# A bias tile loaded as overlapping rows of a table and read backwards, in a one-layer hybrid decoder

## The chip, the core and the metric

The kernel runs on one core of one Trainium2 chip. The metric is the device time of one execution in microseconds, taken as the median over several runs. A core has five engines that run side by side and synchronise with semaphores: TensorE (PE in the profile, with PEld for its weight loads), VectorE (DVE), ScalarE (ACT), GpSimd (POOL) and SyncE (SP). SP and POOL issue the DMA transfers of this kernel; all transfers share 16 DMA engines.

## The reference

One layer of a decoder is computed for 256 tokens of width 1024, in float32. Cut to what matters here:

```python
def hybrid_mixer(x, w_in, b_in, conv_qk, mlstm_norm, rel_bias, w_branch_a, w_branch_b, w_out):
    proj = einsum("bsd,dn->bsn", x, w_in) + b_in
    q_m, k_m, v_m, o_m, i_m, f_m, q_b, k_b, v_b, g_a, g_b = split(proj)
    ...                                            # mLSTM branch (4 heads x 256) -> y_a
    h_b = moba_attention(q_b, k_b, v_b, rel_bias)  # 8 heads x 128 -> y_b
    merged = sigmoid(g_a) * (y_a @ w_branch_a) + sigmoid(g_b) * (y_b @ w_branch_b)
    return merged @ w_out

# with 256 tokens and a block of 256, each query attends its own block only:
rel_own   = q_pos[:, None] - k_pos[None, :]
bias_own  = moveaxis(rel_bias[t5_bucket(rel_own)], -1, 0)     # depends on q_pos - k_pos and the head
logit_own = einsum("bhqd,bhkd->bhqk", q, k) * 128 ** -0.5 + bias_own
logit_own = where(rel_own >= 0, logit_own, -inf)
h_b       = softmax(logit_own) @ v

x = layer_norm(ALPHA * x + mix, ln1_g, ln1_b)
x = layer_norm(ALPHA * x + conv_gated_mlp(x), ln2_g, ln2_b)
```

The bias of a pair of query and key depends on their distance alone, so for one head it is a row of 256 numbers, and a query further on sees that row shifted by one.

## The kernel before

**Weights.** All weights are streamed from DRAM in chunks of 128 x 2048 float32 (1 MB), in the order that `chunk_order` (L45) writes out. Each chunk is split by ACT and DVE (L93, L94) into a rounded part `wh` and a remainder `wl`, and PE makes every product as three matmuls (L147): high by high, low by high, high by low. The main loop (L342) takes one chunk a step: `elem_work(s)` puts the elementwise work of the step on ACT, DVE and POOL, with the split of chunk s + 2 among it; `load(s + 5)` issues a later chunk on SP; then `step_<kind>` issues the chunk's matmuls, and after them the small matmuls of `side_pe`. The order of instructions on each engine is the order in which the program writes them.

**Groups.** The mixer runs in four groups of one mLSTM head and two attention heads. A group has eight chunks (qm, qb, km, kb, vm, vb, ga, gb), and its small work is laid between them by `group_schedule` (L644). For a group that begins at chunk b, the steps that matter here are (groups 0 to 2):

- after the matmuls of chunk b + 5 (vb): the mLSTM scores `pss` (L653) and the logits `psl` of the first head (L755);
- with chunk b + 6 (ga), in this order: `el_w` (L665: ACT makes the decay weights `wt` from the row `nMb`, POOL masks them), `el_l(0)` (L770: DVE adds the bias to the logits and takes the row maximum, L779), the split of vb into `vbh` and `vbl` (L531), `el_e(0)` (ACT's exponentials, L788), `el_s` (L676: scores times weights, ACT's rounded part `sph`), `el_l2(0)` (L790: division by the row sum), `el_s2` (L687: the remainder `spl`);
- after the matmuls of chunk b + 6: the logits of the second head, and `psn` (L691), the mLSTM product, which needs `sph` and `spl`;
- with chunk b + 7 (gb): `el_l(1)` and its followers, and after its matmuls the transposes `pst` of both heads' probabilities (L796).

The last group has the same pieces one step earlier.

**The bias.** `rel_bias_expand` (L554) makes, once, a matmul of the bias table with a one-hot matrix. Its result `ps` (8 heads x 256) holds at column j the bias for distance 255 - j. `elem` copies it, divided by the logit scale, into `ev` (8 x 384), fills the last 128 columns with -1e30 (keys that lie ahead of the query), and stores `ev` as the DRAM tensor `table`.

Each group then needs a tile `toe` of 128 partitions x 2 heads x 256 keys, in which row p is the table's row shifted by p. `copy_band` (L401) writes 128 copies of a table row of 384 behind one another into a DRAM tensor `band`, and `load_band` (L406) reads that back with a row length of 383, so that each row begins one element earlier in its copy. Both are issued on POOL, and the load waits for the copy. Copy and load of group 0 stand right behind the store of `table`. The copy for group g + 1 stands behind the elementwise work of group g's chunk ga; the load for group g + 1, into the same tile `toe`, stands with the second chunk of group g + 1, behind the logits of group g.

**Names in the profile.** L566 is the store of `table`, L403 the copies, L408 the loads, L779 the logits' bias, L672 POOL's mask, L731 POOL's power for the mLSTM norm.

Of the kernel before, what the change touches and what calls it, by code (L numbers as in the profile page):

```python
# [10 lines left out]
F32 = mybir.dt.float32  # L11
# [3 lines left out]
ALU = mybir.AluOpType  # L15
# [3 lines left out]
P = 128  # L19
S = 256  # L20
D = 1024
KT = D // P
NG = 4
# [6 lines left out]
ATT_SCALE = 128.0 ** -0.5  # L30
NEG = -1.0e30
LTOE = 384
# [40 lines left out]
class Kernel:  # L73
# [105 lines left out]
    def run(self):  # L179
        tc, nc, ctx = self.tc, self.nc, self.ctx  # L180
# [3 lines left out]
        dram = ctx.enter_context(tc.tile_pool(name="dram", bufs=1, space=DRAM))  # L184
# [106 lines left out]
        g = nc.gpsimd  # L291
# [34 lines left out]
        for gi in range(NG):  # L326
            self.group_schedule(gi)

        self.bands = [dram.tile([2, P * LTOE], F32, name=f"band{i}") for i in range(NG)]
        self.table = dram.tile([8, LTOE], F32, name="table")  # L330
        self.mrows = dram.tile([4, S], F32, name="mrows")

# [65 lines left out]
        self.pt = [(ap.tile([P, 2, P], F32R, name=f"pth{i}"), ap.tile([P, 2, P], F32R, name=f"ptl{i}"),  # L398
                    ap.tile([P, P], F32, name=f"ptf{i}")) for i in range(2)]

    def copy_band(self, g):  # L401

        self.nc.gpsimd.dma_start(self.bands[g].rearrange("h (p c) -> h p c", p=P),  # L403
                                 self.table[2 * g:2 * g + 2, :].unsqueeze(1).to_broadcast([2, P, LTOE]))

    def load_band(self, g):  # L406
        src = self.bands[g][:, 127:127 + P * (LTOE - 1)].rearrange("h (p c) -> p h c", c=LTOE - 1)
        self.nc.gpsimd.dma_start(self.toe, src[:, :, 0:S])  # L408


    def step_o(self, whl, bo):
# [142 lines left out]
    def rel_bias_expand(self, rel, onehot):  # L554
        nc = self.nc
        st = {}

        def pe():
            st["ps"] = ps = self.ps_side([8, S], "ps_rel")
            nc.tensor.matmul(ps, rel, onehot, start=True, stop=True)  # L560

        def elem():
            ev = self.xp.tile([8, LTOE], F32, name="ev")
            nc.vector.tensor_scalar(ev[:, 0:S], st["ps"], 1.0 / ATT_SCALE, None, op0=ALU.mult)
            nc.vector.memset(ev[:, S:LTOE], NEG)
            nc.gpsimd.dma_start(self.table, ev)  # L566
            self.copy_band(0)
            self.load_band(0)
        self.side_pe.setdefault(4, []).append(pe)
        self.side_elem.setdefault(5, []).append(elem)  # L570
# [73 lines left out]
    def group_schedule(self, g):  # L644
        nc = self.nc
        v, a = nc.vector, nc.scalar
        st = {}
# [122 lines left out]
        def el_l(i):  # L770
            h = 2 * g + i
            ps = st["l", i]
            lg = self.ap.tile([P, 3, P], F32, tag="lg", name=f"lg{h}", bufs=2)
            mx = self.ap.tile([P, 2], F32, tag="mx", name=f"mx{h}", bufs=2)
            sm = self.ap.tile([P, 2], F32, tag="sm", name=f"sm{h}", bufs=2)
            seg = ((lg[:, 0, :], ps[:, 0, 0:P], self.toe[:, i, P:2 * P]),
                   (lg[:, 1:3, :].rearrange("p t c -> p (t c)"), ps[:, 1, :], self.toe[:, i, :]))
            for t, (o, p, tb) in enumerate(seg):
                v.tensor_tensor_reduce(out=o, in0=p, in1=tb, scale=ATT_SCALE, scalar=-3.0e38, op0=ALU.add, op1=ALU.max,  # L779
                                       accum_out=mx[:, t:t + 1])  # L780
            v.tensor_scalar(mx, mx, -1.0, None, op0=ALU.mult)
            st["p", i] = lg
            st["m", i] = seg, mx, sm
# [46 lines left out]
        def at(where, k, f):  # L830
            where.setdefault(b + k, []).append(f)

        if g:
            at(self.side_elem, 1, lambda: self.load_band(g))
        if g < NG - 1:
            at(self.side_elem, 6, lambda: self.copy_band(g + 1))

        o = int(g < NG - 1)
        at(self.side_elem, 3 + o, row_m)
# [4 lines left out]
        if o:  # L844
            self.mixed[b + 6] = lambda w: [el_w, lambda: el_l(0), w[0], lambda: el_e(0), el_s, lambda: el_l2(0),
                                           el_s2] + w[1:]
        else:
            self.mixed[b + 5] = lambda w: [w[0], el_w, lambda: el_l(0), w[1], lambda: el_e(0), el_s,
                                           lambda: el_l2(0), el_s2] + w[2:]
        if g == 0:  # L850
            at(self.side_elem, 6, lambda: self.floor_exp())
        at(self.side_pe, 6 + o, lambda: pe_t(0))
        at(self.side_pe, 6 + o, lambda: pe_t(1))
        self.mixed[b + 6 + o] = lambda w: [lambda: el_l(1), lambda: el_e(1), el_n1] + w + [lambda: el_l2(1), el_n1b]
        at(self.side_pe, 7 + o, pe_y)
        at(self.side_pe, 7 + o, pe_o)
# [445 lines left out]
```

## Time and profile before

| | us |
|---|---|
| median of 3 runs | 485.36 |
| the runs | 491.53, 485.36, 484.46 |
| the profiled execution, whole | 489.01 |
| its span | 487.3 |
| PE busy in the span | 475.9 |
| DVE busy | 371.1 |
| ACT busy | 298.1 |
| POOL busy | 28.8 |

The profile is of one execution. Its span runs from the first to the last instruction, and 1.71 us of that execution lie outside it. Rows of a timeline give the start in us, the length in us, engine, line, operation, output and inputs by the program's names with their shapes, the number of merged instructions, and in brackets the idle time of the engine before them with what ended it. Rows of the chain give start, length and what ran; "issue" is time in which the profile shows no wait that was ended by anything. Rows by stretches give the busy time of PE, PEld, DVE, ACT and POOL with the number of instructions, then the clock that TensorE was granted (1.00 is full), the mean busy share of the DMA engines and GB/s. Rows of DMA issues give the median time from issue to landing last. The starts of PE's matmuls are measured and their ends are modelled, so that one row can reach into the next.

The memory traffic of the bias is small beside the weights: 94.31 MB were moved in all, of which the four copies write 384.0 KB each and the four loads 256.0 KB each.

### The profile page before, as it was taken

Reading aid. Unit: us, or ns where it says so; the run is one execution under the profiler, and the core shown is the slowest. Engines: PE = TensorE matmul, PEld = TensorE weight load, DVE = VectorE, ACT = ScalarE, POOL = GpSimd, SP = SyncE. Lnnn points to the kernel's source line nnn. Section 1 sums busy time; section 2 is a strip of 40 time slices with the busy share of each in tenths; the row PEclk is TensorE's granted clock in tenths of the full one; section 3 lists DMA queues with packets and bytes.
Section 4 is the critical chain, followed back from the end, with each engine's and each line's share of the span. In section 5 each row is a group of like instructions: output and inputs, shape, how many; then the busy total and the mean of one; then the engine's idle time right before and its main releaser. Section 6 shows DMA issues by size and latency. Waiting matters only on the chain.

```text
span 487.3 us, 9421 instructions
## 1 busy us (share of the span) xinstructions
PE 475.9 (98%) x3831; PEld 460.2 (94%) x3831; DVE 371.1 (76%) x666; ACT 298.1 (61%) x509; POOL 28.8 (6%) x45
## 2 busy tenths in 40 slices
PE   7999989999999999999999999999999999999994
PEld 5999989999999999999999999999999999999984
DVE  5779948796779686986666799888677667767886
ACT  5579656686569656867655541776445554556871
POOL 0501012001100110001100002000000000000000
PEclk9999998999999999999999999999999999999998
DMA  7976664466435754544875480736554565555202
GB/s 226 290 303 239 199 235 134 168 231 217 166 145 210 239 157 153 202 169 162 319 284 174 174 310 38 297 136 225 208 178 174 204 223 173 174 196 230 93 1 87
DMA packets 21030, 94.31 MB, mean 194 GB/s; under 512 B 4947, under 2 KB 7905, under 8 KB 11129
## 3 DMA queue, kind: packets, MB, share of 16 engines
q1 hardware_dynamic: 16714, 87.61, 50.2%
q0 software_dynamic: 4272, 6.09, 4.0%
q8 instruction: 30, 0.49, 0.4%
q14 instruction: 14, 0.11, 0.1%
HBM read 92.59 MB, written 2.64 MB: 195 GB/s over the span
## 4 chain that ended last, share of the span: by engine, by line
PE 83%; DMA 6%; issue 4%; DVE 3%; ACT 1%; SPq 1%; POOL 0%; DVEq 0%; ACTq 0%; POOLq 0%
PE ps_up L147 25%; PE ffn L147 12%; PE ps_gb L147 5%; PE mix L147 4%; PE ps_wb L147 4%; PE ps_wa L147 4%; PE ps_ga L147 3%; PE ps_kb L147 3%; PE ps_qm L147 3%; PE ps_qb L147 3%; PE ps_vm L147 3%; PE ps_vb L147 3%; PE ps_km L147 3%; DMA raw<-in_wst_dram 3%; DMA xraw<-in_xt_dram 2%
## 5 line engine op out<-in xcount | busy, mean ns | idle before, releaser
L94 DVE TENSOR_TENSOR wl<-raw,wh 128x1024 fp32r<-128x1024 f32 (+4 forms) x147 | 179.3, 1257 | 26.9 <-ACT wh L93 24.2
L93 ACT CAST wh<-raw 128x1024 fp32r<-128x1024 f32 (+4 forms) x147 | 151.7, 1080 | 8.5 <-DMA raw<-in_wst_dram 6.1
L147 PE MATMUL ps_up<-x1h,wl 128*128 128x256 f32 x320 | 88.5, 276 | 0.0
L147 PE MATMUL ps_up<-x1h,wh 128*128 128x256 f32 x320 | 88.4, 276 | 0.0
L147 PE MATMUL ps_up<-x1l,wh 128*128 128x256 f32 x320 | 88.4, 276 | 0.0
L147 PEld LDWEIGHTS ps_up<-x1l,wh 128*128 128x128 f32 x320 | 60.1, 188 | 0.4
L147 PEld LDWEIGHTS ps_up<-x1h,wh 128*128 128x128 f32 x320 | 60.1, 188 | 0.3
L147 PEld LDWEIGHTS ps_up<-x1h,wl 128*128 128x128 f32 x320 | 60.1, 188 | 0.0
L1080 DVE SCALAR_TENSOR_TENSOR cu<-ps_up,vec,cu 128x255 f32<-128x255 f32 (+1 forms) x80 | 33.0, 475 | 20.4 <-ACT cu L1076 20.4
L147 PE MATMUL ffn<-wh,hl 128*128 128x512 f32 (+2 forms) x94 | 35.5, 378 | 0.0
L147 PE MATMUL ffn<-wl,hh 128*128 128x512 f32 (+2 forms) x94 | 35.5, 377 | 0.0
L147 PE MATMUL ffn<-wh,hh 128*128 128x512 f32 (+2 forms) x94 | 35.3, 375 | 0.0
L93 ACT CAST hh<-cu 128x256 fp32r<-128x256 f32 x22 | 8.9, 406 | 40.4 <-DVE cu L1091 40.4
L1076 ACT ACTIVATE cu<-ps_up,vec 128x256 f32<-128x256 f32 x40 | 16.7, 470 | 22.5 <-PE ps_up L147 22.5
L147 PEld LDWEIGHTS ffn<-wh,hl 128*128 128x128 f32 x94 | 17.7, 188 | 3.2
L147 PEld LDWEIGHTS ffn<-wh,hh 128*128 128x128 f32 x94 | 17.7, 188 | 3.1
L147 PEld LDWEIGHTS ffn<-wl,hh 128*128 128x128 f32 x94 | 17.7, 188 | 3.0
L147 PE MATMUL ps_gb<-xth,wh 128*128 128x256 f32 x64 | 18.0, 282 | 0.0
L147 PE MATMUL ps_qm<-xth,wh 128*128 128x256 f32 x64 | 18.0, 281 | 0.0
L147 PE MATMUL ps_ga<-xth,wh 128*128 128x256 f32 x64 | 18.0, 281 | 0.0
L147 PE MATMUL ps_gb<-xtl,wh 128*128 128x256 f32 x64 | 17.9, 280 | 0.0
L147 PE MATMUL mix<-wh,mgh 128*128 128x256 f32 x64 | 17.8, 279 | 0.0
(344 smaller groups left out, 1454.6 us busy)
## 6 DMA issues: line engine op xcount, KB each, us to landing
raw<-in_wst_dram SPq DMA_DIRECT2D x77, 1024.0 KB, 4.9
raw<-in_wst_dram SPq DMA_DIRECT2D x8, 256.0 KB, 4.3
lnrow<-in_rows_dram POOLq DMA_DIRECT2D x4, 512.0 KB, 6.5
band<-table POOLq DMA_DIRECT2D x4, 384.0 KB, 11.2
xraw<-in_xt_dram SPq DMA_DIRECT2D x8, 128.0 KB, 4.0
toe<-band POOLq DMA_DIRECT2D x4, 256.0 KB, 4.6
xtok<-in_x_dram POOLq DMA_DIRECT2D x1, 1024.0 KB, 7.8
sgb<-in_wst_dram SPq DMA_DIRECT2D x4, 128.0 KB, 4.1
```

The lines of the kernel that those rows point to most:

```text
L93: self.nc.scalar.copy(wh, raw)
L94: self.nc.vector.tensor_sub(wl, raw, wh.bitcast(F32))
L147: self.nc.tensor.matmul(ps, a[i], b[i], start=start and i == 0, stop=stop and i == 2)
L1076: act.activation(cu[:, j, :], ps[:, j, :], AF.Copy, scale=tap(2, j))
L1080: v.scalar_tensor_tensor(cu[:, j, o:], ps[:, j, :S - o], tap(t, j), cu[:, j, o:], op0=ALU.mult, op1=ALU.add)
```

## The change

The copies in DRAM are gone. `ev` is built the other way round: its first 128 columns are -1e30, and column 128 + m holds the bias for distance m, which DVE gets by reading the matmul's result backwards in PSUM. `load_band` reads `table` itself: partition p gets the 256 elements from column 1 + p on, for both heads, so that the 128 rows overlap in all but one element each. That tile has the keys in reversed order: element 255 - k of row p is the bias for distance 128 + p - k, which is query 128 + p and key k. The new helper `backward` makes a view with step -1 over 256 elements, and `el_l` gives this view of `toe` to the logits instruction; the first query block takes the last 128 elements of the view, as before.

The store of `table` on POOL is followed directly by the load of group 0. The loads of groups 1 to 3 stay where they were. Sizes, numbers and order of all other instructions are as before.

```diff
-        self.bands = [dram.tile([2, P * LTOE], F32, name=f"band{i}") for i in range(NG)]
         self.table = dram.tile([8, LTOE], F32, name="table")
...
-    def copy_band(self, g):
-
-        self.nc.gpsimd.dma_start(self.bands[g].rearrange("h (p c) -> h p c", p=P),
-                                 self.table[2 * g:2 * g + 2, :].unsqueeze(1).to_broadcast([2, P, LTOE]))
+    def backward(self, t):
+        return bass.AP(t.tensor, t.offset + S - 1, [list(t.ap[0]), [-1, S]])

     def load_band(self, g):
-        src = self.bands[g][:, 127:127 + P * (LTOE - 1)].rearrange("h (p c) -> p h c", c=LTOE - 1)
-        self.nc.gpsimd.dma_start(self.toe, src[:, :, 0:S])
+        t = self.table[2 * g:2 * g + 2, 1:S + 1].unsqueeze(0)
+        rows = bass.AP(t.tensor, t.offset, [[1, P], *t.ap[1:]])
+        self.nc.gpsimd.dma_start(self.toe, rows)
...
             ev = self.xp.tile([8, LTOE], F32, name="ev")
-            nc.vector.tensor_scalar(ev[:, 0:S], st["ps"], 1.0 / ATT_SCALE, None, op0=ALU.mult)
-            nc.vector.memset(ev[:, S:LTOE], NEG)
+            nc.vector.tensor_scalar(ev[:, P:LTOE], self.backward(st["ps"]), 1.0 / ATT_SCALE, None, op0=ALU.mult)
+            nc.vector.memset(ev[:, 0:P], NEG)
             nc.gpsimd.dma_start(self.table, ev)
-            self.copy_band(0)
             self.load_band(0)
...
-            seg = ((lg[:, 0, :], ps[:, 0, 0:P], self.toe[:, i, P:2 * P]),
-                   (lg[:, 1:3, :].rearrange("p t c -> p (t c)"), ps[:, 1, :], self.toe[:, i, :]))
+            toe = self.backward(self.toe[:, i, :])
+            seg = ((lg[:, 0, :], ps[:, 0, 0:P], toe[:, P:2 * P]),
+                   (lg[:, 1:3, :].rearrange("p t c -> p (t c)"), ps[:, 1, :], toe))
...
-        if g < NG - 1:
-            at(self.side_elem, 6, lambda: self.copy_band(g + 1))
```

## The prediction

> **What bounds the kernel now.** I read the page's head first, then busy time by stretches (span, then busy us of PE, PEld, DVE, ACT, POOL; PEclk; DMA share; GB/s), then the chain that ended last, then each engine's timeline around the one place where PE stops.
>
> ```profile
> span 487.3 us, 9421 instructions
> PE 475.9 (98%) x3831; PEld 460.2 (94%) x3831; DVE 371.1 (76%) x666; ACT 298.1 (61%) x509; POOL 28.8 (6%) x45
> ```
> ```profile
> 65.00:71.00 6.00, 6.00 (x54) 5.95 (x53) 1.01 (x7) 2.21 (x4) 2.15 (x3) 1.00 0.75 240
> 71.00:74.00 3.00, 0.85 (x4) 0.41 (x2) 2.06 (x7) 2.55 (x8) 0.00 (x0) 0.88 0.14 54
> 74.00:76.00 2.00, 2.00 (x9) 2.00 (x10) 1.86 (x2) 1.06 (x2) 0.00 (x0) 0.50 0.12 51
> ...
> 94.00:480.00 386.00, 386.00 (x3148) 375.96 (x3147) 298.29 (x515) 235.65 (x392) 15.23 (x20) 1.00 0.52 186
> ```
> From 94 to 480 us PE is busy for 386.00 of 386.00 us at full granted clock: nothing that shortens other engines there can shorten the kernel. The exception is 71 to 76: PE works 0.85 us of 3, and the next 2 us are granted a clock of 0.50. The chain (start, length) says whose fault it is:
>
> ```profile
> 47.77 1.12 POOL band L403
> 48.89 15.95 issue
> 64.86 5.21 DMA toe<-band
> ...
> 71.09 0.34 DVE vbl L94
> ...
> 73.40 0.56 DVE spl L689
> 73.96 0.04 issue
> 74.00 1.87 PE psn L147 x7
> 75.88 5.91 PE ps_gb L147 x48
> 81.79 0.65 PE pst L799 x6
> ```
> ```profile
> 124.34 0.22 PE psl L760 x2
> 124.56 1.07 PE psn L147 x9
> 125.63 5.46 PE ps_gb L147 x48
> 131.09 0.65 PE pst L799 x6
> ```
> The 15.95 us of "issue" are the flight of the first band copy. The copy and the load after it bring the first bias tile at 70.07 us; DVE's logits wait for it, the chain ends in psn, and PE stands. Group 1 (second fence) has the same PE work without that wait.
>
> ```profile
> 62.92 2.36 DVE L94 TENSOR_TENSOR wl<-raw,wh 128x1024 fp32r<-128x1024 f32 x2 [0.25 <-ACT wh L93]
> 70.24 0.29 DVE L779 CUSTOM_DVE_ANT_0 lg<-psl,toe 128x128 f32<-128x128 f32 x1 [4.96 <-DMA toe<-band]
> ```
> ```profile
> 64.72 0.38 PE L760 MATMUL psl<-kbf,qbf 128*128 128x128 f32 x2
> ```
> ```profile
> 70.76 0.38 PE L760 MATMUL psl<-kbf,qbf 128*128 128x128 f32 x2
> 73.16 0.49 PE L147 MATMUL psn<-vmh,sph 128*128 128x258 f32 x1 [2.01 <-ACT sph L683]
> ```
> DVE is idle for 4.96 us before the logits; its own work was done at 62.92 + 2.36 = 65.28, and PE's logits product at 64.72 + 0.38 = 65.10.
>
> **The change part by part.** *The first copy goes.* The load of the first tile takes the copy's place in POOL's queue, at 47.77, behind the same table store. What the load costs there, with overlapping rows as source, has no row. Its nearest rows (KB, us from issue to landing):
>
> ```profile
> lnrow<-in_rows_dram POOLq DMA_DIRECT2D x4, 512.0 KB, 6.5
> band<-table POOLq DMA_DIRECT2D x4, 384.0 KB, 11.2
> ```
> ```profile
> band<-table POOLq DMA_DIRECT2D x1, 384.0 KB, 16.8
> ```
> Lower bound: 5.2, the load of before (5.21 in the chain; the same destination, size and row length). Upper bound: 16.8, the slowest copy out of the same table in the very stretch where the load will now run. I take 5.2 to 6.5, since lnrow too has all partitions read the same few KB; landing is at 53.0 to 54.3. Even 16.8 gives 47.77 + 16.8 = 64.6, before 65.28. So the logits start at 65.28 at every price between the bounds; a slower reversed PSUM read into ev (or its memset, which only moves) has the same 11 us of cover.
>
> *What is late next.* DVE runs logits, vbl, scores, spl in that order.
>
> ```profile
> 66.87 0.35 ACT L93 CAST vbh<-ps_vb 128x256 fp32r<-128x256 f32 x1
> ```
> ```profile
> 67.09 0.42 POOL L672 TENSOR_SCALAR_AFFINE_SELECT wt<-wt 128x256 f32<-128x256 f32 x1 [1.48 <-ACT wt L671]
> ```
> The logits took 71.09 - 70.24 = 0.85, so they end at 66.13. vbl needs vbh, at 67.22; the scores need the mask, at 67.51. If vbl starts at 67.24, and vbl to the end of spl keeps its length of 73.96 - 71.09 = 2.87, spl is there at 70.1. PE finishes the second logits product at 70.76 + 0.22 = 70.98 (two issues took 0.22 in group 1). So psn's operands are 0.9 us early, and PE has no wait. That is the margin on which the forecast stands.
>
> *The sum.* psn starts at 70.98. In group 1 psn's start to pst's start takes 131.09 - 124.56 = 6.53. So pst starts at 77.51 instead of 81.79: **4.28 us** less, of which 2.18 is the gap (73.16 - 70.98) and 2.10 the wait inside psn and the matmuls at the lower clock. Behind it PE has no waits, so the whole tail moves with it. Weights don't object: the split that DVE does next is of the weights two chunks ahead, and it moves up with spl.
>
> ```profile
> 74.14 2.36 DVE L94 TENSOR_TENSOR wl<-raw,wh 128x1024 fp32r<-128x1024 f32 x2 [0.19 <-ACT wh L93]
> ```
>
> On that clock the Trainium skill, "TensorE: Matmul & The Clock Gate", Part 1, says the clock drops after an idle window of about 3.4 us. The trace disagrees: 0.50 was granted right behind a gap of 2.2 us. Were the rule right, the low clock would have another cause and could stay; that is the second rival below.
>
> *The other copies and loads.* Three later copies (L403) leave POOL and the DMA engines. Nothing waits for them: the next tile's load is
>
> ```profile
> 82.04 0.90 POOL L408 DMA_DIRECT2D toe<-band  x1
> ```
> and its reader comes a whole group later, past 118. Cover is over 30 us, so both the copies and the new loads count nothing, even at 16.8.
>
> *Reversed reads of the bias tile*, 16 instructions (min/median/max ns), no row of before reads backwards:
>
> ```profile
> L779 DVE CUSTOM_DVE_ANT_0 lg<-psl,toe x16: 282/356/422, 70.2 to 217.9; 128x128 f32<-128x128 f32 x8, 128x256 f32<-128x256 f32 x8
> ```
> ```profile
> 46.62 0.68 DVE L608 TENSOR_TENSOR_SCAN gates<-ones,gates 4x256 f32<-4x256 f32 x1
> ```
> Lower bound: unchanged, 0.28 and 0.42 us (0.14 us for 128 columns more, 1.1 ns a column; a gain has no room, as the PSUM operand is still read forwards at one column a step). Upper bound: the slowest DVE row over 256 columns, the scan, 0.68 against 0.42: about 1.6 times, +0.43 us for a pair. I take unchanged, since the pace is a column at a time already. At the upper bound it is hidden too: in group 0 the pair ends at 66.6, before vbh; in the others DVE normalises its logits well before PE transposes them (group 1: 126.92 + 0.55 = 127.47 against 131.09, 3.62 us):
>
> ```profile
> 126.92 0.55 DVE L794 TENSOR_SCALAR lg<-lg,sm 128x128 f32<-128x128 f32 x2
> ```
>
> Sum: span 487.3 - 4.28 = 483.0. The profiled execution took 489.01, 1.71 outside the span; 484.7 after. The median of the runs shown is 485.36 (484.46 to 491.53), so against it the forecast is **481.1 us**, 0.9% less.
>
> **Rivals.** *Late load.* POOL's load now starts while DVE is full, where the old load started with DVE idle:
>
> ```profile
> 47.80:61.30 13.50, 13.50 (x122) 13.50 (x120) 13.38 (x24) 9.05 (x16) 1.09 (x1) 1.00 0.65 218
> 65.30:70.10 4.80, 4.80 (x45) 4.80 (x44) 0.00 (x0) 1.91 (x4) 1.85 (x3) 1.00 0.79 265
> ```
> If POOL's load only gets on when DVE goes idle (65.28), it lands 5.2 us later, at 70.5, against 70.07: before's time, no gain, 485.4. For it: the copy in the busy stretch was the slowest, 16.8. Against it: the copy did land while DVE was busy. It decides from a landing later than 66.4 + 0.9 = 67.3 (vbl needs 67.24 and 0.85 of logits before it), 19.5 us after issue; no row is that long. The Trainium skill, "SBUF — State Buffer", Who interferes with whom, states such a block of POOL's descriptor writing, but only by DVE's two-port modes; no run here shows which. Chance 0.08.
>
> *Half the gain.* Either the low clock of 74 to 76 comes anyway, or another operand of psn (ACT's chain behind the nMb row, with 0.9 us to spare) is late: only about the gap's 2.18 is won, 483.2. Against: groups 1 to 3 run the same work at full clock without a wait. Chance 0.10.
>
> *Slower: reversed reads cost several times as much.* Each pair of reads (0.28 + 0.42) grows by x, and a group has two in line ahead of the transposes. A group then loses 2x less its cover: 3.62 in groups 1 to 3 (group 3 taken like 1), in group 0
>
> ```profile
> 78.66 0.55 DVE L794 TENSOR_SCALAR lg<-lg,sm 128x128 f32<-128x128 f32 x2
> ```
> 79.21, moved by the 3.86 that spl moves (73.96 to 70.1) to 75.35, against pst at 77.51: 2.16. Together 8x - 13.0. The gain of 4.28 is eaten at x = 2.16, a pair four times as long; over 2% slower needs x = 3.4. At six times, x = 3.5: 28.0 - 13.0 = 15.0 lost, 485.36 - 4.28 + 15.0 = 496.1. For it: no row reads backwards. Against: the slowest row is 1.6 times. Chance 0.04.
>
> *It doesn't do what it says*: the first load is held on POOL by a wait that the diff doesn't show, up to about 64.86, where the old load was issued: 485.4, chance 0.03. Against it: in the diff the load reads only the table, and DVE had not read that tile before.
>
> **How the numbers follow.** Forecast 0.75, rivals 0.08, 0.10, 0.04, 0.03. The forecast's own range is 479.7 to 482.5: 0.9 to each side, by which the two closest runs shown differ (485.36 - 484.46), and 0.1% (0.5) more, since three runs are few. The whole range reaches on through half a gain (483.2) to no gain with the same 0.5, 479.7 to 485.9, and leaves out the slow rival (0.04). About 2% (9.7 us) is what a measurement of this kernel can tell from no change: no case reaches -9.7, so faster 0.02; the slow rival, partly, gives slower 0.04; within 0.94.
>
> **What would show it.** Right: toe lands near 53; DVE's first logits start at 65.3 with no wait on a DMA; PE has no idle before group 0's psn and PEclk stays 1.00 through 76; pst of group 0 starts near 77.5; L779 keeps 282/422 ns; L403's DMAs are gone, and the stretch that was 94 to 480 still has PE full. Wrong: a wait of logits on toe, L779 beyond 1 us, or a new PE wait in any group.

## The result, and the profile after

| | before | changed |
|---|---|---|
| median of 22 runs each, us | 486.77 | 484.73 |
| lowest to highest | 484.46 to 492.96 | 484.29 to 485.43 |
| runs above 488.5 | 9 of 22 | 0 of 22 |
| the profiled execution | 489.01 | 485.31 |
| its span | 487.3 | 483.6 |

The ratio of the times is 0.9949 with a 95% interval of 0.9926 to 0.9973: 0.5% faster, within the 2% that count as no change. The ratio leaves out runs more than 1.5% above a kernel's fastest; kernels whose first tile comes in time have no such long runs, even with the copies in place (e3 and e5 below), so on the whole set of runs the change is worth a little more (the means are 488.23 and 484.83, 0.7%). The forecast of 481.1 us was too low by 3.6, and its gain of 4.28 us too large for the medians, which lie 2.04 apart. Beside that the spread of the runs has changed: 8.5 us before, 1.1 us after.

In the trace of the changed kernel, however, nearly every step of the prediction stands. First POOL's timeline, then DVE's, around group 0 (start, length, what ran, idle time before it):

```profile
48.08 0.77 POOL L406 DMA_DIRECT2D toe<-table  x1 [2.63 <-DMA table<-ev]
66.49 0.42 POOL L669 TENSOR_SCALAR_AFFINE_SELECT wt<-wt 128x256 f32<-128x256 f32 x1 [17.63 <-ACT wt L668]
```
```profile
65.50 0.28 DVE L777 CUSTOM_DVE_ANT_0 lg<-psl,toe 128x128 f32<-128x128 f32 x1
...
66.65 0.42 DVE L94 TENSOR_TENSOR vbl<-ps_vb,vbh 128x256 fp32r<-128x256 f32 x1 [0.31 <-ACT vbh L93]
...
69.06 0.56 DVE L686 TENSOR_TENSOR spl<-wt,sph 128x384 fp32r<-128x384 f32 x1
```
The DMA issues of 44 to 72 us give the load's flight, and the tile's view its readers:

```profile
toe<-table POOLq DMA_DIRECT2D x1, 256.0 KB, 3.7
```
```profile
L777 DVE CUSTOM_DVE_ANT_0 lg<-psl,toe x16: 284/356/421, 65.5 to 214.1; 128x128 f32<-128x128 f32 x8, 128x256 f32<-128x256 f32 x8
```
The load lands 3.7 us after its issue at 48.08, at 51.8; the logits start at 65.50 with no idle time of DVE in front; spl is ready at 69.62. PE, in the chain and in the stretches:

```profile
71.23 0.22 PE psl L757 x2
71.45 1.07 PE psn L147 x9
72.53 5.46 PE ps_gb L147 x48
77.99 0.66 PE pst L797 x6
```
```profile
71.00:74.00 3.00, 3.00 (x29) 3.00 (x28) 2.96 (x14) 1.03 (x5) 0.00 (x0) 1.00 0.25 44
74.00:76.00 2.00, 2.00 (x20) 2.00 (x19) 1.93 (x13) 2.00 (x4) 0.00 (x0) 1.00 0.95 393
```
PE doesn't stop, the clock stays at 1.00, and pst starts at 77.99 instead of 81.79: 3.80 us earlier, and the span is 3.7 us shorter. So the question is not where the gain went in the trace, but why a gain of 3.7 us in one pair of executions is 2 us between the medians.

### The profile page after: what moved, and what is told of

Read it like the earlier page. It is cut to its first block, busy times and chain, and to the rows that moved or that the text cites. A ratio compares the mean times of both kernels' runs of the same rounds, so it can differ in the third digit from the quotient of the medians.

```text
span 483.6 us, 9414 instructions
## 1 busy us (share of the span) xinstructions
PE 474.1 (98%) x3831; PEld 458.8 (95%) x3831; DVE 371.1 (77%) x666; ACT 297.9 (62%) x509; POOL 23.7 (5%) x41
## 4 chain that ended last, share of the span: by engine, by line
PE 92%; DMA 5%; DVE 1%; ACT 1%; SPq 1%; issue 0%; DVEq 0%; ACTq 0%
PE ps_up L147 25%; PE ffn L147 13%; PE ps_ga L147 5%; PE ps_kb L147 5%; PE ps_qb L147 5%; PE ps_gb L147 5%; PE ps_vm L147 5%; PE mix L147 5%; PE ps_vb L147 5%; PE ps_wb L147 5%; PE ps_wa L147 5%; PE ps_km L147 4%; PE ps_qm L147 4%; DMA raw<-in_wst_dram 2%; DMA sigo<-in_wst_dram 1%; PE psn L147 1%
## 5 line engine op out<-in xcount | busy, mean ns | idle before, releaser
L147 PE MATMUL ps_qm<-xth,wl 128*128 128x256 f32 x64 | 17.9, 280 | 0.4 <-DVE wl L94 0.4
L147 PE MATMUL ps_qb<-xth,wh 128*128 128x256 f32 x64 | 17.8, 278 | 0.0
```

What stands on the lines that cost most here:

```text
L147: self.nc.tensor.matmul(ps, a[i], b[i], start=start and i == 0, stop=stop and i == 2)
```

## The experiments

The theory: the kernel before has its stall in different sizes from one execution to the next, from nothing to more than in the profile shown; the change takes all of it away, and nothing else. The rival: the stall is much the same each time, and the changed kernel gives part of the gain back (reversed reads, the new load). Each kernel ran 12 times. Medians of the kernel before in the three comparisons were 487.57 (e1 to e4), 485.42 (e5 to e8) and 485.81 (e9, e10).

| | what | median | lowest to highest | above 488.5 |
|---|---|---|---|---|
| e1 | before, unchanged | 485.54 | 484.31 to 491.97 | 4 |
| e2 | copies kept, order reversed | 484.86 | 484.40 to 491.17 | 1 |
| e8 | e2 once more | 486.94 | 484.75 to 491.57 | 5 |
| e3 | changed, copies put back unread | 484.97 | 484.38 to 486.57 | 0 |
| e4 | changed, first load at 66.8 us | 490.65 | 489.68 to 491.42 | 12 |
| e5 | before, copies' dimensions swapped | 484.63 | 484.39 to 485.94 | 0 |
| e6 | changed, load at 62.6, new tile | 486.72 | 486.30 to 488.84 | 1 |
| e7 | changed, load at 64.5, new tile | 488.46 | 487.83 to 491.70 | 6 |
| e9 | e6 without the new tile | 485.37 | 484.69 to 486.71 | 0 |
| e10 | e7 without the new tile | 488.75 | 486.88 to 490.64 | 7 |

**e1: the kernel before, once more.** No edit.

> The kernel before, unchanged, to see how its stall at 71 us varies between executions. Theory A (the stall's length varies with the landing of the first band copy and with the clock behind the gap): times spread over 484.5 to 493 us as in the runs of before, the longer ones at a lower mean clock, and this profile has another stall than the 2.2 us gap and the 0.50 stretch of the first profile; the tile lands at another time than 70.07 us. Theory B (the stall is the same in every execution, and the changed kernel lost some of its gain elsewhere): the profile repeats the stall within 0.3 us, and the spread has another place.

Its profile is of an execution of 484.36 us, and the stall is not there. Chain, then DVE's timeline:

```profile
70.40 0.22 PE psl L760 x2
70.62 1.07 PE psn L147 x9
71.69 5.46 PE ps_gb L147 x48
77.15 0.66 PE pst L799 x6
```
```profile
66.55 0.29 DVE L779 CUSTOM_DVE_ANT_0 lg<-psl,toe 128x128 f32<-128x128 f32 x1 [1.79 <-DMA toe<-band]
```
The copy's flight was 15.9 us instead of 16.8, the table's store 1.7 instead of 2.9, and the whole chain began 1.0 us sooner, so the tile landed at 66.4 us instead of 70.1; DVE waits 1.79 us instead of 4.96, and the slack that the changed kernel has in front of psn swallows that. Of the 12 runs, eight lie between 484.31 and 487.27 at a mean granted clock of 0.995 to 0.998, four between 490.19 and 491.97 at 0.990 to 0.992, and none between the two groups. The same split runs through all 105 runs of the kernel before whose clock is on record, in e1 and in the three comparisons: the 71 up to 487.81 us have a mean clock of 0.995 or more, the 34 from 488.00 on have 0.994 or less. The theory holds; the rival, which wanted the same stall within 0.3 us, does not. No run above 489.81 us was profiled, so the make-up of the longest ones is argued from their times and clocks.

**e2 and e8: the reversal alone.** The copies are in place and used (put back as in e3); table and reads are reversed as in the change. The edit to the changed kernel's load:

```diff
     def load_band(self, g):
-        t = self.table[2 * g:2 * g + 2, 1:S + 1].unsqueeze(0)
-        rows = bass.AP(t.tensor, t.offset, [[1, P], *t.ap[1:]])
+        t = self.bands[g][:, 0:1]
+        rows = bass.AP(t.tensor, t.offset + 1, [[LTOE + 1, P], list(t.ap[0]), [1, S]])
```

> The copies in DRAM stay, only the order is reversed: the table backwards, the tile from the copies with a row length of 385, the logits read backwards. Theory A: times and spread like the kernel before (485 to 487 us median, some runs above 490), L779's counterpart at 0.28 and 0.42 us, DVE's wait on the tile of about 5 us. Rival (reversed reads cost something that eats part of the gain): 1 to 2 us above before.

> The kernel with the copies kept and only the order reversed, once more, since 1 of its 12 runs lay above 489 where the kernel before has some 4 in 10. If that was chance: 3 to 7 of 12 runs above 489. If the second transfer is quicker with rows 385 apart than 383 apart (it landed in 3.3 us against 3.7 to 5.2): again 0 to 2.

Both have the long runs of the kernel before, 1 and 5 of 12. That e2 had only one may have been chance, as e8's five suggest, but it is not shown: e2 and e8 ran on two chips, beside 16 of 35 and 8 of 35 long runs of the kernel before. In e2's profile the copy was quick (13.1 us) and so was the load behind it (3.3); in e8's they took 16.8 and 5.5, so the new row distance does not make the load quicker by itself. The reversed reads cost nothing (the view of the tile in e2):

```profile
L784 DVE CUSTOM_DVE_ANT_0 lg<-psl,toe x16: 283/356/421, 65.4 to 213.7; 128x128 f32<-128x128 f32 x8, 128x256 f32<-128x256 f32 x8
```
e8's profile, of 486.66 us, shows the case between: PE waits 1.12 us and then 0.35 inside psn, and the clock stays.

```profile
72.03 0.39 PE L147 MATMUL psn<-vmh,sph 128*128 128x258 f32 x1 [1.12 <-ACT sph L687]
```
```profile
74.00:76.00 2.00, 2.00 (x20) 2.00 (x20) 1.97 (x7) 0.00 (x0) 0.00 (x0) 1.00 0.13 53
```

**e3: the copies' traffic without the wait.** In the changed kernel:

```diff
             nc.gpsimd.dma_start(self.table, ev)
+            self.copy_band(0)
             self.load_band(0)
...
+        if g < NG - 1:
+            at(self.side_elem, 6, lambda: self.copy_band(g + 1))
```

> The changed kernel with the four copies put back at their old places, where nothing reads them. Theory A: 484.7 us like the changed kernel, within 0.5, small spread: the copies cost only through the wait for the first of them; the first load is issued 1.1 us later and lands before 65 us. Rival (the copies' traffic, not the wait, is what costs): half or more of the difference back, 486 to 487 us.

484.97: the four copies cost next to nothing when nothing waits for them. But the first load, issued at 47.23 behind the copy, took long:

```profile
toe<-table POOLq DMA_DIRECT2D x1, 256.0 KB, 17.1
```
It landed at 64.3, 0.4 us before the logits at 64.74. So the late load of the prediction's first rival exists, through the copy's company and not through a busy DVE, and four of the 12 runs (485.49 to 486.57) lie above all runs of the changed kernel.

**e4: a late tile without any copy.** In the changed kernel the first load moves behind POOL's mask of group 0.

```diff
             nc.gpsimd.dma_start(self.table, ev)
-            self.load_band(0)
...
             st["wt"] = wt
+            if g == 0:
+                self.load_band(0)
```

> The changed kernel with group 0's load moved behind POOL's mask of group 0 (issue at about 67 us), so that the tile is late with no copy at all. Theory A: it lands at about 72.3 us, PE stands some 4.4 us before group 0's scores product instead of 2.2, the clock drops behind it, and time is 7 to 10 us over the changed kernel (491 to 495), with a spread of several us again. Theory B (a late tile costs the same 2 to 3 us whatever the gap): 487 to 488.

```profile
74.04 0.47 PE L147 MATMUL psn<-vmh,sph 128*128 128x258 f32 x1 [2.80 <-ACT sph L681]
```
```profile
74.00:76.00 2.00, 1.79 (x7) 1.50 (x8) 1.81 (x4) 1.95 (x3) 0.00 (x0) 0.55 0.00 0
```
All 12 runs carry the stall, at a mean clock of 0.990 to 0.994, and 490.65 is 5.9 us over the changed kernel: the stall is made by the late tile alone. The expected 491 to 495 was a little high, since the load took only 4.2 us and PE's gap came to 3.0 us (from 71.08, the end of psl's issues, to 74.04) and not to 4.4.

**e5: the copy spread over the DMA engines.** Why is the copy so slow? In the profile of before there is a stretch in which it is alone on the DMA engines:

```profile
53.00:53.50 0.50, 0.50 (x7) 0.50 (x6) 0.50 (x2) 0.00 (x0) 0.00 (x0) 1.00 0.12 46
```
A mean busy share of 0.12 over 16 engines is as much as two engines kept full. The copy's outermost dimension is the two heads. On that the Trainium skill, "DMA: Bandwidth & Descriptors", Rules for kernel authors, says that an outermost dimension of fewer than 16 confines a transfer to as many engines; two heads, two engines, and the trace agrees. The test swaps the dimensions in the kernel before and changes nothing else:

```diff
-        self.nc.gpsimd.dma_start(self.bands[g].rearrange("h (p c) -> h p c", p=P),
-                                 self.table[2 * g:2 * g + 2, :].unsqueeze(1).to_broadcast([2, P, LTOE]))
+        self.nc.gpsimd.dma_start(self.bands[g].rearrange("h (p c) -> p h c", p=P),
+                                 self.table[2 * g:2 * g + 2, :].unsqueeze(0).to_broadcast([P, 2, LTOE]))
```

> The kernel before; only the copies' dimensions are swapped, so that the 128 partitions and not the two heads come first. Theory A1 (the first copy is slow because it runs on two of the 16 DMA engines: share 0.12 and 46 GB/s while it is alone at 53 us): it now lands in 4 to 8 us instead of 13 to 17, the first tile lands before 62 us, and time is 484.7 us within 0.5, all runs below 487, with copy, second transfer and forward reads all in place. Rival (the copy is slow because of its rows or because DRAM is written): landing stays above 11 us and time at 485 to 488 with runs above 490.

```profile
46.04 0.76 POOL L403 DMA_DIRECT2D band<-table  x1 [1.46 <-DMA table<-ev]
51.12 0.73 POOL L408 DMA_DIRECT2D toe<-band  x1 [4.32 <-DMA band<-table]
```
```profile
band<-table POOLq DMA_DIRECT2D x1, 384.0 KB, 4.8
toe<-band POOLq DMA_DIRECT2D x1, 256.0 KB, 5.4
```
The copy lands in 4.8 us instead of 16.8, copy and load together are done at 56.5, and the kernel with all four copies runs in 484.63, against 484.73 for the changed one. All that the change brings lies in this one wait.

**e6, e7, e9, e10: how the time follows the gap.** The load of the changed kernel is held on POOL by a two-element copy until vml (e6, e9) or the gate columns (e7, e10) are there. e6 and e7 write it into a new tile, e9 and e10 into the tile that the load then overwrites. e7's edit; e6 has the same three lines behind the split of vm, with the copy reading vml. The last two lines are e10's, in place of the new tile and its copy:

```diff
             nc.gpsimd.dma_start(self.table, ev)
-            self.load_band(0)
...
             if g == 0:
                 self.gate_cols()
+                gate = self.mp.tile([P, 2], F32, name="gate")
+                nc.gpsimd.tensor_copy(gate, self.gcol[:, 0, 0:2])
+                self.load_band(0)
...
+                nc.gpsimd.tensor_copy(self.toe[:, 0, 0:2], self.gcol[:, 0, 0:2])
+                self.load_band(0)
```

> The changed kernel with group 0's load held on POOL until DVE has made vml (about 63 us), a small copy on POOL being the hold. Theory A: issue at about 63.7, landing at 69, PE's gap before the scores product about 1 us, clock kept: 485.2 to 486.5 us, no run above 489. Theory B (any gap costs the clock): 488 or more.

> The same with the load held until ACT has copied the gate columns (about 64.2 us). Theory A: issue at about 64.8, landing at 70 as in the profile of before, gap about 2 us; times in two bands, near 486.5 with the clock kept and near 489 to 490 with it lost. Theory B (the cost grows with the gap alone): one band at 486.5 to 487.5.

> As e6, but the hold writes two numbers into the tile that the load then overwrites, so that no new tile moves the addresses of others (in e6 and e7 six PE chunks of 48 took 5.66 us instead of 5.45, 1.2 us in all). If the new tile caused that: all such chunks at 5.44 to 5.48 again, gap about 0.5 us, clock kept, 485.3 us within 0.5. If the late load itself caused it: 5.66 stays, and 486.5 to 487.

> As e7 without the new tile. Theory A (clock lost only behind a gap of about 2 us): gap 1.5 to 2 us, most runs at 486.5 to 487.3 with the clock kept, up to 4 of 12 near 490 with it lost, few between. Theory B (cost grows with the gap alone): all runs within 1.5 us of each other.

e6 came out 0.2 us above the 485.2 to 486.5 that were expected, with a gap of only 0.34 us. Its chain shows why, beside that of e9:

```profile
72.36 5.66 PE ps_gb L147 x48
78.03 0.65 PE pst L800 x6
78.68 5.66 PE ps_qm L147 x48
```
```profile
72.41 5.46 PE ps_gb L147 x48
```
With the new tile, six chunks of 48 matmuls take 5.65 to 5.66 us instead of 5.44 to 5.46, 1.2 us in all; without it all are at 5.44 to 5.48, and the median falls from 486.72 to 485.37. So the 8-byte tile was the cost, not the late load; how it costs is open (see the last section). e6 and e7 are read with 1.2 us off; e9 and e10 are the clean pair.

e7's median of 488.46 is 487.3 without that, but its runs don't fall into two clear bands: nine lie at 487.83 to 489.06 with a mean clock of 0.995 to 0.998, two at 490.11 and 490.92 with 0.994 and 0.992, and one at 491.70 with 0.995, for which the theory has no account.

e10's profile shows the loss of the clock apart from the gap. PE waits 1.75 us and 0.34 inside psn, and psn still runs at its usual pace; then the next chunk takes 7.06 instead of 5.46:

```profile
72.48 0.39 PE L147 MATMUL psn<-vmh,sph 128*128 128x258 f32 x1 [1.75 <-ACT sph L681]
```
```profile
73.33 1.11 PE psn L147 x7
74.45 7.06 PE ps_gb L147 x48
81.50 0.66 PE pst L798 x6
```
```profile
74.00:76.00 2.00, 2.00 (x13) 2.00 (x12) 2.00 (x5) 0.39 (x1) 0.00 (x0) 0.60 0.00 0
76.00:78.00 2.00, 2.00 (x12) 2.00 (x12) 1.93 (x16) 1.38 (x6) 0.00 (x0) 0.55 0.61 98
```
Its runs are five at 486.88 to 487.37 (mean clock 0.995 to 0.997) and seven at 488.61 to 490.64 (0.990 to 0.994): two bands, as the theory has it, though more in the upper one than the four expected. The profiles in order of the time at which the first tile landed (e7's times with what the new tile costs; "psl to pst" runs from the start of PE's second logits product to that of the transposes):

| profile | tile landed, us | PE's waits at psn, us | psl to pst, us | PEclk from 74 to 76 | that execution, us |
|---|---|---|---|---|---|
| e1 | 66.4 | 0 | 6.91 | 1.00 | 484.36 |
| e9 | 67.4 | 0.34 | 7.51 | 1.00 | 484.96 |
| e8 | 69.0 | 1.47 | 8.91 | 1.00 | 486.66 |
| e7 | 69.4 | 1.79 | 9.45 | 1.00 | 488.56 |
| e10 | 69.4 | 2.09 | 11.15 | 0.60 | 488.61 |
| before | 70.1 | 2.01 and a part inside psn | 11.03 | 0.50 | 489.01 |
| e4 | 71.0 | 2.97 | 11.83 | 0.55 | 489.81 |

The stall sets in between landings at 66.4 and 67.4 us, where the prediction's first rival had put it (67.3). In the profiles with the clock kept, the stretch from psl to pst grows by the wait and 0.3 to 0.5 us more (0.75 in e7, with one of the slow chunks in it); where the clock was lost, it grows by about 2 us more than the wait. Together with the time at which PE reached psl (70.24 to 70.86 us), this stretch accounts for the difference of each execution to e1 within 0.1 us, but for e7, in which the slow chunks come on top. One profile each doesn't make a threshold: the clock was kept at 1.79 us of waits and lost at 2.09, and in e4, whose profile shows 2.97, the mean clock is low in all 12 runs.

## Why the prediction was right in its steps and wrong in its size

- **What bounds the kernel.** Right for the execution that was profiled: one wait, for the first tile. e5 takes that wait away by another way and gets the same time.
- **The load's price.** Too high, without effect: 3.7 us, below the lower bound of 5.2, and covered either way. The upper bound of 16.8 was the price of two engines, as e5 shows; it was no property of the stretch.
- **What is late next.** Right, with more room than worked out: spl is ready 1.83 us before psn, not 0.9, since ACT too began sooner (the vb split at 66.27 instead of 66.87) and psn starts 0.47 later than was worked out.
- **The other copies, the reversed reads.** Right: nothing (e3, e2).
- **The sum in the trace.** Nearly right: psl's end to pst took 6.54 us, 6.53 was worked out. pst came 0.48 later than forecast. Of that, 0.31 is PE reaching psl later (71.07 instead of 70.76 in the timelines); 0.01 is the stretch behind it (6.54 against 6.53), and 0.16 was an error of the sum, which added a length from the chain to a start from the timeline, while the chain puts the same psl 0.16 later (71.23 against 71.07 in the changed kernel). So the stall of that execution was worth 4.12 us, not 4.28 (11.03 - 6.91 in the table above). In the changed kernel's execution PE also waited 0.4 us for the first weights of qm, which the first profile doesn't have, and that is about the size of the later start (waits of PE, us and times):

```profile
PE ps_qm L147 <- DVE wl L94: 0.4, 1, 0.4
```
- **The step that failed** is the last: "The median of the runs shown is 485.36, so against it the forecast is 481.1 us". It took the stall of one execution, 4.28 us, off a median of executions with other stalls. Taken off its own execution it gives 489.01 - 4.28 = 484.73, which is the median measured; that it agrees to the last digit is luck, since that stall was worth 4.12 us and the executions of the changed kernel differ by 1.1. What the runs showed in place of the step: the stall of before is 0 in one execution and 4 us in another, and its median has little of it. Its lowest runs are those without a stall (e1: 484.36), so no forecast should have gone below them by removing the stall. The sign was there to be seen: the profiled execution, at 489.01, lay 3.65 and 4.55 us above two of the three runs shown, about as much as the whole stall.
- **The rivals.** None came true. Half the gain is what the medians look like, but for another reason: the gap and the low clock both went, while more than half of the executions of before had not lost the clock (71 of the 105 above). That 484.73 lies inside the whole range, which these rivals had stretched to 485.9, is luck. The late load appears only with the copies beside it (e3).

Not settled is why the copy's flight differs by some 3 us between executions (13.1 us in e2, 15.9 in e1, 16.8 in e8 and in the first profile), and with it the share of long runs (9 of 22, 16 of 35, 4 of 12, 8 of 35 and 5 of 23 runs above 488.5 for the kernel before, in comparisons on several chips). The two engines also carry their part of the weights, which is an argument and was not tried.

## What to carry to other kernels

A stall that hangs on one transfer has no single size: compare the profiled execution with the other runs before its stall is taken off their median, and take the fastest runs as the floor for what its removal can reach, as long as some of them are free of it (e4's fastest, 489.68, is not such a floor). A long transfer with a low DMA share is worth a look at its outermost dimension; here two swapped dimensions were worth as much as doing without the copies. And an edit that adds a small tile can move the time by itself, so an experiment should write into what is there.

## What the runs showed of the hardware that was not expected

The clock did not fall with the gap but some time after it, and not at a fixed one: in e10 PE stopped at 70.57, worked again from 72.48 at full pace but for a wait of 0.34 us, and lost the clock at 74.4, 3.8 us after it had stopped; in e4 it was 3.1 us after the stop, in the first profile 2.3. Once lost, it stayed at 0.50 for 3.4 us in all three: in e10, 0.60 and 0.55 over 2 us each are 1.6 and 1.8 us at half clock. That is a price of 1.7 us on top of the gap (e10's next chunk took 7.06 instead of 5.46). The Trainium skill, "TensorE: Matmul & The Clock Gate", Part 1, describes a window that runs freely of the work. The varying delay agrees with that. The 3.4 us of idle time that the same part asks for do not agree: gaps of 2.0 and 2.1 us were followed by the low clock in the first profile and in e10's.

PE's pace fell with an extra tile of 8 bytes: 5.66 against 5.45 us for 48 matmuls of the same shapes at full clock, in six chunks of e6 and of e7. The operands of these matmuls, xth, xtl, wh and wl, lie ahead of the new tile in the kernel's layout and keep their addresses; what moves are tiles behind it, such as wt, lg and spl. Why that slows PE is open.

Reading a float32 tile or PSUM backwards on DVE costs nothing: 284/356/421 ns against 282/356/422 forwards for the tile, and 405 against 404 ns for the one read of 8 x 256 from PSUM. The loads with overlapping rows were somewhat slower where both can be compared at ease: in groups 2 and 3 they took 5.4 and 5.3 us, against 4.0 and 3.8 from the copies in the kernel before. Nothing waited for them, and whether the overlap is the cause was not tried.
